# Sending one split output block: which rows go through which transfer engine, and by which queue

## The chip, the core and the metric

The kernel runs on one core of a Trainium2 chip. The core has five instruction engines: TensorE (PE, matmuls into PSUM), VectorE (DVE), ScalarE (ACT), GpSimd (POOL) and SyncE (SP). Data moves between HBM and the on-chip memory SBUF through 16 transfer engines, which serve two queues here: SyncE's (q1 in the profile) and GpSimd's (q0). A transfer is cut into packets, each transfer engine works through its own share, and when its share has landed it counts the transfer's semaphore up by one. "Landing records" in this text are the times of these counts, sixteen for a transfer.

The metric is the time of one execution on the device in microseconds. Before the change three runs took 299.66, 299.67 and 300.48 us, a median of 299.67 us.

## What is computed

```python
def setup_inputs():
    batch, n_heads, seq_t, seq_s, channels = 8, 12, 512, 512, 64
    return {
        "x": np.random.randn(batch, n_heads, seq_t, channels).astype(np.float32),
        "y": np.random.randn(batch, n_heads, seq_s, channels).astype(np.float32),
    }

def reference(x, y):
    return np.einsum('bhtc,bhsc->bhts', x, y).astype(np.float32)
```

For each of the 96 pairs of batch and head, the 512 x 64 matrix x is multiplied with the transposed 512 x 64 matrix y. Inputs are 25.2 MB, the output is 100.7 MB.

## The kernel before

**Tiles and stages.** The 96 heads are worked on as 6 groups of 16. One group of x, and one of y, is one load of 2 MB into one of five slots (`load`, L156). `compress` (L165) rounds a loaded slot to bf16, `mix` (L189) and `transposes` (L204) bring the channels onto the partitions. The output leaves as 48 blocks of 2 MB; block `o` has 128 rows of 4096 numbers (16 KB), a row for each partition. For each block `result` (L363) has TensorE make two half blocks in two PSUM tiles (`products`, `four`) and ScalarE copy them to a slot (L370), and then `store` (L356) has SyncE send the slot to HBM (L361). A slot is filled again when its store has landed. The matmuls run in one loop, `all_products` (L244), while the other engines' instructions are written out one after another. `emit` (L111) records what each instruction reads and writes and puts the waits in front of it.

**The split block.** One block, number `SPLIT` = 41 of 0 to 47, is sent in two parts. `store` sends only its odd rows, 64 runs of 16 KB, as half a store (1024 KB, L359 to L361). Its 64 even rows are computed again in another layout and sent apart, by transfers that do not use all sixteen transfer engines alike:

- `pick` (L266) has VectorE collect the columns of x for these rows into `picked`, in 18 banks of 96 columns. The table `APART` (L53) has one entry for each group of rows: `p` is the first partition that the group gets (further ones follow in steps of 4), `many` the number of partitions, and `first` the first row. Each partition gets `MANY` = 2 runs, run `j` of partition `e` being row `first + j * many + e`. From row `REST` = 60 on, four rows are cut into 16 units of 1024 numbers (4 KB), one for each of 16 partitions, in the last two banks (L283).
- `pieces` (L291) has TensorE multiply the banks behind blocks 41 and 45 (`BEHIND`) and VectorE and ScalarE copy the results into `kept`.
- `send` (L331) issues the transfers. Entries with `many` = 4 go by SyncE (two transfers of 4 partitions with 2 runs, 128 KB each), those with 11 by GpSimd (two of 11 partitions with 2 runs, 352 KB each). The 16 units go by SyncE as one transfer (64 KB, L349).
- `step` (L320) is a small transfer by GpSimd's queue, of 5 rows with two pieces of 64 bytes. It reads x into a tile that nobody uses. It is issued once at the start (L395) and once between the two 11-row transfers.

**What follows.** Behind all this work stands the end of a block of instructions whose engines are gathered by GpSimd (`tile_critical`, L388): every engine ends with a drain, and GpSimd then lets SyncE issue the last store, that of block 47 (L439). While that store runs, VectorE waits for all other transfers (L433).

Of the kernel before, what the change touches and what calls it, by code (L numbers as in the profile page):

```python
# [9 lines left out]
def kernel(  # L10
# [22 lines left out]
    nc = tc.nc  # L33
    B, H, T, C = x.shape
    _, _, S, _ = y.shape
# [4 lines left out]
    NG = B * H // G  # L40
    NH = 2 * NG
    V = G // 4
    K = 8
    E = R // K
    D = 32
# [4 lines left out]
    MANY = 2  # L50
    BANKS = MANY * K + 2
    BEHIND = {SPLIT: range(3), SPLIT + 4: range(3, 5)}
    APART = ((32, 4, 0), (33, 4, 8), (52, 11, 16), (53, 11, 38))  # L53
    REST = 60
    TURN = 4 * V
    fp32 = mybir.dt.float32
    bf16 = mybir.dt.bfloat16
# [4 lines left out]
    xv = x.rearrange("b h t c -> (b h t c)").rearrange("(g p n) -> g p n", p=P, n=R * C)  # L62
# [18 lines left out]
    spare = sb.tile([P, 2, D], fp32, name="spare")  # L81
# [7 lines left out]
    def need(name, points, known_by=None, held=None):  # L89

        best = {}
        for p, v in points:
            if known[name].get(p, 0) < v:
                best[p] = max(best.get(p, 0), v)
        for p, v in list(best.items()):
            if any(snaps[q, w].get(p, 0) >= v for q, w in best.items() if q != p):
                del best[p]
        if known_by is not None:
            assert all(p in dict(known_by) and v <= dict(known_by)[p] for p, v in best.items())
        for p, v in best.items():  # L100
            if held is not None:
                held.append((p, v))
            elif known_by is None:
                engines[name].wait_ge(sems[p], v)  # L104
            known[name][p] = v
            for q, w in snaps[p, v].items():
                known[name][q] = max(known[name].get(q, 0), w)
# [3 lines left out]
    def emit(name, make, reads=(), writes=(), dma=None, lane=None, known_by=None, held=None):  # L111

        points = [writer[r] for r in (*reads, *writes) if r in writer]
        points += [v for w in writes for v in readers.get(w, ())]
        if name == "pool" and name in ticks:
            points.append((name, ticks[name]))
        need(name, points, known_by, held)
        p, step = (lane or name, 1) if dma is None else (f"dma{dma}", 16)
        if p not in sems:
            sems[p] = tc.alloc_semaphore(p)  # L120
        if held is not None:
            held.append(make)
        elif make is not None:
            make().then_inc(sems[p], step)
        at = (p, ticks.get(p, 0) + step)
        ticks[p] = at[1]
        snaps[at] = {**known[name], p: at[1]}
        if dma is None:
            for q in lanes.get(name, (name,)):
                snaps[at][q] = ticks.get(q, 0)  # L130
        for r in reads:
            readers.setdefault(r, []).append(at)
        for w in writes:
            writer[w], readers[w] = at, []
# [21 lines left out]
    def load(n):  # L156
        i = loaded[n] = slot()
        emit(
            "sp",
            lambda: nc.sync.dma_start(slots[i], (yv if n % 2 else xv)[n // 2]),  # L160
            writes=both(i),
            dma=i,
        )
# [98 lines left out]
    kept = keep[:, :BANKS * S].bitcast(fp32)  # L262
    runs = kept[:, :MANY * K * S].rearrange("p (j n) -> p j n", j=MANY)
    picked = keep[:, 3 * NG * R // 2 * D:].bitcast(bf16)[:, :BANKS * 96].rearrange("p (b m) -> p b m", b=BANKS)

    def pick():  # L266

        half, h = divmod(SPLIT % (2 * V), V)
        xT = xTs[half].bitcast(bf16).rearrange("p (k h q u) -> p k h q u", k=K, h=V, u=2)[:, :, h, :, 0]
        under = [("yb", 1, b, ch) for b in range(NG - 3, NG - 1) for ch in range(2)]  # L270
        for at, (p, many, first) in enumerate(APART):
            emit(
                "dve",
                lambda: nc.vector.tensor_copy(  # L274
                    picked[:, :MANY * K, p:p + 4 * many - 3:4].rearrange("p (j k) e -> p j k e", j=MANY),
                    xT[:, :, first:first + MANY * many].rearrange("p k (j e) -> p j k e", j=MANY),
                ),
                [("xT", half)],
                [("picked", at)] + (under if at == 0 else []),
            )  # L280
        emit(
            "dve",
            lambda: nc.vector.tensor_copy(  # L283
                picked[:, MANY * K:, 32::4].rearrange("p b (r c) -> p b r c", c=4),
                xT[:, :, REST:].rearrange("p (c b) r -> p b r c", b=2),
            ),
            [("xT", half)],
            [("picked", len(APART))],
        )

    def pieces(o):  # L291
# [4 lines left out]
        for g in BEHIND[o]:  # L296
# [3 lines left out]
            def make(banks=banks, pm=pm):  # L300
# [8 lines left out]
            emit(  # L309
                "pe", make, [("picked", at) for at in range(len(APART) + 1)] + [("yT", half)],  # L310
                [("pm", pm)], held=held[o],
# [5 lines left out]
            )  # L317
        need("pe", [v for pm in range(2) for v in readers[("pm", pm)]], held=held[o])

    def step():  # L320

        emit(
            "pool",
            lambda: nc.gpsimd.dma_start(  # L324
                spare[0:17:4, :, :D // 2], xv[0, 0:5].rearrange("p (a b c) -> p a b c", a=2, c=D)[:, :, 0, :D // 2]
            ),
            writes=["spare"],
            dma="step",
        )

    def send():  # L331

        dst = ov[SPLIT // V, SPLIT % V][:, 0]
        for p, many, first in APART:
            name = "sp" if many == 4 else "pool"
            if first == APART[-1][2]:
                step()
            emit(
                name,
                lambda: engines[name].dma_start(  # L340
                    dst[first:first + MANY * many].rearrange("(j e) n -> e j n", j=MANY),
                    runs[p:p + 4 * many - 3:4],
                ),
                reads=[("xk", g) for g in range(NG - 1)],
                dma="corner" if name == "sp" else "side",
            )
        emit(
            "sp",
            lambda: nc.sync.dma_start(  # L349
                dst[REST:].rearrange("r (c n) -> (r c) n", c=4), kept[32:93:4, MANY * K * S:]  # L350
            ),
            reads=[("xk", g) for g in range(NG - 1)],
            dma="corner",
        )

    def store(o, s):  # L356
# [6 lines left out]
    def result(o, s):  # L363

        for k in range(0, K, 4):
            pm = k // 4
            products(o, k)
            emit(
                "act",
                lambda: nc.scalar.activation(  # L370
                    slots[s][:, k * S:(k + 4) * S], pms[pm].rearrange("p j s -> p (j s)"), COPY
                ),
                [("pm", pm)],
                [("slot", s, pm)],
                lane=f"ev{(2 * o + pm) % TURN}",
            )
        if o < V * NH - 1:
            store(o, s)
# [9 lines left out]
    with tc.tile_critical(sync_engine=mybir.EngineType.Pool) as work:  # L388
        for at in (TURN - 2, TURN - 1):
            sems[f"ev{at}"] = tc.alloc_semaphore(f"ev{at}")  # L390
            ticks[f"ev{at}"] = 1
            nc.scalar.sem_inc(sems[f"ev{at}"], 1)
        for g in range(SLOTS):
            load(g)
        step()  # L395
        for half, name in enumerate(("dve", "pool")):
            emit(
                name,
                lambda: engines[name].memset(xbs[half], 0.0),  # L399
                writes=[("xb", half, part) for part in range(4)],  # L400
            )
        front = []
        for n in range(2 * NG):
            if n == 11:
                result(3, slot())
            compress(n)
            mix(n // 4, "pool", n % 4)
            if n == 4:
                transposes(0)
            if n < 5:  # L410
                load(n + SLOTS)
            elif n in (6, 8):
                load(n // 2 + 7)
            elif n < 10:
                front.append(slot())
            if n > 7 and n < 11:
                result(n - 8, front[n - 8])
            if n == 9:
                transposes(1)
        prepare(2)  # L420
        for o in range(V, V * NH):
            result(o, slot())
            if o in BEHIND:
                pieces(o)
            if o == max(BEHIND):
                send()
            if o % V == V - 1:
                prepare(o // V + 2)
            if o == SPLIT - V - 1:
                pick()  # L430
        all_products()
# [43 lines left out]
```

## Time and profile before

| what | us |
|---|---|
| median of three runs | 299.67 |
| profiled execution | 299.64 |
| its span, first to last instruction | 297.8 |
| ACT busy | 214.2 |
| DVE busy | 159.5 |
| PE busy | 140.5 |
| POOL busy | 58.5 |

The span is what the profiler saw between the first and the last instruction; the execution lasts 1.84 us longer. Busy shares are averages over the whole span, so that the last 30 us, where the split block is sent, have to be read by themselves: in the timeline (start, length, engine, line) and in the issues of transfers, which the page lists with size and median time from the issue to the landing:

```profile
out_dram<-slot SPq DMA_DIRECT2D x47, 2048.0 KB, 20.8
out_dram<-slot SPq DMA_DIRECT2D x1, 1024.0 KB, 18.4
out_dram<-keep POOLq DMA_DIRECT2D x2, 352.0 KB, 9.6
out_dram<-keep SPq DMA_DIRECT2D x2, 128.0 KB
out_dram<-keep SPq DMA_DIRECT2D x1, 64.0 KB
spare<-in_x_dram POOLq DMA_DIRECT2D x2, 0.6 KB, 7.5
```

A store takes some 20 us to land because three or four others stand before it in SyncE's queue; one 2 MB store lands every 4.9 us.

### The profile page before, as it was taken

Reading aid. Unit: us, or ns where it says so; the run is one execution under the profiler, and the core shown is the slowest. Engines: PE = TensorE matmul, PEld = TensorE weight load, DVE = VectorE, ACT = ScalarE, POOL = GpSimd, SP = SyncE. Lnnn points to the kernel's source line nnn. Section 1 sums busy time; section 2 is a strip of 40 time slices with the busy share of each in tenths; the row PEclk is TensorE's granted clock in tenths of the full one; section 3 lists DMA queues with packets and bytes.
Section 4 is the critical chain, followed back from the end, with each engine's and each line's share of the span. In section 5 each row is a group of like instructions: output and inputs, shape, how many; then the busy total and the mean of one; then the engine's idle time right before and its main releaser. Section 6 shows DMA issues by size and latency. Waiting matters only on the chain.

```text
span 297.8 us, 1269 instructions
## 1 busy us (share of the span) xinstructions
PE 140.5 (47%) x396; PEld 38.2 (13%) x402; DVE 159.5 (54%) x81; ACT 214.2 (72%) x111; POOL 58.5 (20%) x27
## 2 busy tenths in 40 slices
PE   0000040456656553866565667556657556754200
PEld 0000010111111111111111111111111112211000
DVE  2157897999839594906809339167095435103000
ACT  1665676999999988686868686868686865597700
POOL 3399999991000000000000000000000000002000
PEclk9999999978799998565786775786775686799855
DMA  7999999999999999999999999999999999999997
GB/s 271 433 427 436 429 427 429 427 422 442 429 431 422 440 429 430 425 438 429 431 425 439 429 431 429 433 429 427 429 436 425 429 427 427 425 422 431 416 429 315
DMA packets 8794, 125.85 MB, mean 423 GB/s; under 512 B 1100, under 2 KB 1100, under 8 KB 1116
## 3 DMA queue, kind: packets, MB, share of 16 engines
q1 hardware_dynamic: 8632, 125.11, 98.8%
q0 software_dynamic: 160, 0.72, 0.6%
q14 instruction: 2, 0.02, 0.0%
HBM read 25.17 MB, written 100.66 MB: 422 GB/s over the span
## 4 chain that ended last, share of the span: by engine, by line
DMA 54%; ACT 28%; issue 5%; PE 4%; DVE 3%; ACTq 1%; SPq 0%; POOLq 0%
DMA out_dram<-slot 41%; ACT slot L370 25%; DMA slot<-in_y_dram 7%; DMA slot<-in_x_dram 6%; DVE keep L144 3%; ACT keep L142 3%; PE pm L238 2%; PE pm L303 1%; ACTq L388 1%; SPq L160 0%; ACTq L104 0%; SPq L470 0%; POOLq L388 0%; POOLq L459 0%
## 5 line engine op out<-in xcount | busy, mean ns | idle before, releaser
L370 ACT ACTIVATE slot<-pm 128x2048 f32<-128x2048 f32 x96 | 173.8, 1897 | 41.6 <-DMA out_dram<-slot 35.3
L238 PE MATMUL pm<-yT,xT 128*128 128x512 bf16 x378 | 134.1, 496 | 133.6 <-ACT slot L370 91.9
L209 DVE STREAM_TRANSPOSE xT<-xb 128x2048 uint32<-128x2048 uint32 x12 | 46.7, 3895 | 68.5 <-PE pm L238 66.2
L238 PEld LDWEIGHTS pm<-yT,xT 128*128 128x128 bf16 x384 | 35.9, 113 | 231.7 <-ACT slot L370 129.1
L142 ACT ACTIVATE keep<-slot 128x4096 bf16<-128x4096 f32 (+1 forms) x12 | 36.5, 3041 | 21.2 <-DMA slot<-in_x_dram 16.1
L144 DVE COPY xb<-keep 32x2048 bf16<-32x2048 bf16 x36 | 46.9, 1302 | 1.0
L144 DVE CAST keep<-slot 64x2048 bf16<-64x2048 f32 x12 | 36.2, 3015 | 16.9 <-DMA slot<-in_y_dram 16.7
L340 POOL DMA_DIRECT2D out_dram<-keep x2 | 1.1, 566 | 204.4 <-ACT keep L142 204.4
L144 POOL COPY xb<-keep 32x2048 bf16<-32x2048 bf16 x12 | 36.2, 3021 | 9.0 <-ACT keep L142 8.2
L218 DVE STREAM_TRANSPOSE yT<-keep 128x1024 uint32<-128x1024 uint32 x12 | 23.1, 1926 | 0.0
L144 DVE COPY keep<-pm 96x2048 f32<-96x2048 f32 x3 | 6.9, 2286 | 24.7 <-PE pm L303 24.7
L144 POOL CAST keep<-slot 64x2048 bf16<-64x2048 f32 x6 | 17.8, 2974 | 1.3 <-DMA slot<-in_y_dram 0.8
L303 PE MATMUL pm<-yT,keep 128*96 128x512 bf16 x18 | 6.4, 500 | 4.3 <-ACT slot L370 4.3
L142 ACT ACTIVATE keep<-pm 96x2048 f32<-96x2048 f32 (+1 forms) x2 | 2.9, 1448 | 2.8 <-PE pm L303 2.8
L303 PEld LDWEIGHTS pm<-yT,keep 128*96 128x96 bf16 x18 | 2.3, 151 | 8.1 <-issue 3.6
L399 DVE MEMSET xb<- 128x2048 uint32 x1 | 1.8, 1765 | 1.4 <-PEq L459 1.4
L142 ACT ACT_TABLE_LOAD x1 | 1.3, 1283 | 1.0 <-PEq L459 1.0
L399 POOL MEMSET xb<- 128x2048 uint32 x1 | 1.8, 1824 | 0.0
L324 POOL DMA_DIRECT2D spare<-in_x_dram x2 | 1.2, 620 | 1.2 <-POOLq L388 1.2
L274 DVE COPY keep<-xT 128x64 bf16<-128x64 bf16 (+1 forms) x4 | 0.8, 322 | 0.0
L283 DVE COPY keep<-xT 128x32 bf16<-128x32 bf16 x1 | 0.3, 260 | 0.0
L459 POOL MEMSET const-float32-0.0<- 128x1 f32 x1 | 0.1, 93 | 0.2 <-issue 0.2
(3 smaller groups left out, 0.3 us busy)
## 6 DMA issues: line engine op xcount, KB each, us to landing
out_dram<-slot SPq DMA_DIRECT2D x47, 2048.0 KB, 20.8
slot<-in_x_dram SPq DMA_DIRECT2D x6, 2048.0 KB, 17.6
slot<-in_y_dram SPq DMA_DIRECT2D x6, 2048.0 KB, 20.8
out_dram<-slot SPq DMA_DIRECT2D x1, 1024.0 KB, 18.4
out_dram<-keep POOLq DMA_DIRECT2D x2, 352.0 KB, 9.6
out_dram<-keep SPq DMA_DIRECT2D x2, 128.0 KB
out_dram<-keep SPq DMA_DIRECT2D x1, 64.0 KB
spare<-in_x_dram POOLq DMA_DIRECT2D x2, 0.6 KB, 7.5
```

Of the source, the lines that this page charges most:

```text
L142: lambda: nc.scalar.activation(dst, src, COPY)
L144: else engines[name].tensor_copy(dst, src),
L209: lambda: nc.vector.transpose(xTs[half].rearrange("p (k r e) -> p k e r", k=K, e=E), xbs[half].rearrange("p (k e c) -> p k e c", k=K, e=E),),
L218: lambda: nc.vector.transpose(yTs[half].rearrange("p (r j) -> p j r", r=D), ybs[half][b].rearrange("p (j c) -> p j c", c=D),),
L238: last = nc.tensor.matmul(pms[pm][:, b, :], xT[:, 4 * pm + b, h, :], yT[:, h * S:(h + 1) * S], start=True, stop=True,)
L274: lambda: nc.vector.tensor_copy(picked[:, :MANY * K, p:p + 4 * many - 3:4].rearrange("p (j k) e -> p j k e", j=MANY), xT[:, :, first:first ...
L303: last = nc.tensor.matmul(pms[pm][:96, b, :], picked[:, bank, :], yT[:, h * S:(h + 1) * S], start=True, stop=True,)
L324: lambda: nc.gpsimd.dma_start(spare[0:17:4, :, :D // 2], xv[0, 0:5].rearrange("p (a b c) -> p a b c", a=2, c=D)[:, :, 0, :D // 2]),
L340: lambda: engines[name].dma_start(dst[first:first + MANY * many].rearrange("(j e) n -> e j n", j=MANY), runs[p:p + 4 * many - 3:4],),
L370: lambda: nc.scalar.activation(slots[s][:, k * S:(k + 4) * S], pms[pm].rearrange("p j s -> p (j s)"), COPY),
L388: with tc.tile_critical(sync_engine=mybir.EngineType.Pool) as work:
L399: lambda: engines[name].memset(xbs[half], 0.0),
```

## The change

The table `APART` gets five entries and two new columns: `j`, the first run of the group's partitions, and `runs_each`, how many runs each has. The first two groups (rows 0 to 15, by SyncE) stay as they are. Rows 16 to 27 now go as 12 partitions with one run, rows 28 to 38 as 11 partitions with one run, rows 39 to 60 as 11 partitions with two runs, each as one transfer by GpSimd. The last three rows (61 to 63) are cut into 12 units of 4 KB and go by GpSimd too, where before four rows went as 16 units by SyncE. `step` becomes `to_engine(n, at)`, of `n` rows instead of 5: with 4 rows at the start, with 5, 5 and 4 rows in front of the last three transfers. The two 352 KB transfers thus become one of 192 KB, one of 176 KB and one of 352 KB, and the 64 KB transfer one of 48 KB. GpSimd issues seven transfers behind the matmuls instead of three, SyncE two instead of three. `pick` has one copy more, and its last one covers 12 partitions instead of 16.

```diff
-    APART = ((32, 4, 0), (33, 4, 8), (52, 11, 16), (53, 11, 38))
-    REST = 60
+    APART = ((32, 4, 0, 2, 0), (33, 4, 0, 2, 8), (48, 12, 0, 1, 16), (52, 11, 1, 1, 28), (53, 11, 0, 2, 39))
+    REST = 61
...
-        for at, (p, many, first) in enumerate(APART):
+        for at, (p, many, j, runs_each, first) in enumerate(APART):
             emit(
                 "dve",
                 lambda: nc.vector.tensor_copy(
-                    picked[:, :MANY * K, p:p + 4 * many - 3:4].rearrange("p (j k) e -> p j k e", j=MANY),
-                    xT[:, :, first:first + MANY * many].rearrange("p k (j e) -> p j k e", j=MANY),
+                    picked[:, j * K:(j + runs_each) * K, p:p + 4 * many - 3:4].rearrange(
+                        "p (j k) e -> p j k e", j=runs_each
+                    ),
+                    xT[:, :, first:first + runs_each * many].rearrange("p k (j e) -> p j k e", j=runs_each),
                 ),
...
-                picked[:, MANY * K:, 32::4].rearrange("p b (r c) -> p b r c", c=4),
+                picked[:, MANY * K:, 48::4].rearrange("p b (r c) -> p b r c", c=4),
...
-    def step():
+    def to_engine(n, at=0):
 
         emit(
             "pool",
             lambda: nc.gpsimd.dma_start(
-                spare[0:17:4, :, :D // 2], xv[0, 0:5].rearrange("p (a b c) -> p a b c", a=2, c=D)[:, :, 0, :D // 2]
+                spare[at:at + 4 * n - 3:4, :, :D // 2],
+                xv[0, 0:n].rearrange("p (a b c) -> p a b c", a=2, c=D)[:, :, 0, :D // 2],
             ),
-            writes=["spare"],
+            writes=[("spare", at)],
             dma="step",
         )
 
     def send():
 
         dst = ov[SPLIT // V, SPLIT % V][:, 0]
-        for p, many, first in APART:
+        ready = [("xk", g) for g in range(NG - 1)]
+        for at, (p, many, j, runs_each, first) in enumerate(APART):
             name = "sp" if many == 4 else "pool"
-            if first == APART[-1][2]:
-                step()
+            if name == "pool" and first > 16:
+                to_engine(16 - many, at - 2)
             emit(
                 name,
                 lambda: engines[name].dma_start(
-                    dst[first:first + MANY * many].rearrange("(j e) n -> e j n", j=MANY),
-                    runs[p:p + 4 * many - 3:4],
+                    dst[first:first + runs_each * many].rearrange("(j e) n -> e j n", j=runs_each),
+                    runs[p:p + 4 * many - 3:4, j:j + runs_each],
                 ),
-                reads=[("xk", g) for g in range(NG - 1)],
+                reads=ready,
                 dma="corner" if name == "sp" else "side",
             )
-        emit(
-            "sp",
-            lambda: nc.sync.dma_start(
-                dst[REST:].rearrange("r (c n) -> (r c) n", c=4), kept[32:93:4, MANY * K * S:]
+        to_engine(4, 3)
+        emit(
+            "pool",
+            lambda: nc.gpsimd.dma_start(
+                dst[REST:].rearrange("r (c n) -> (r c) n", c=4), kept[48:93:4, MANY * K * S:]
             ),
-            reads=[("xk", g) for g in range(NG - 1)],
-            dma="corner",
+            reads=ready,
+            dma="side",
         )
...
-        step()
+        to_engine(4)
```

## The prediction

> **What bounds the kernel now.** I read the busy slices and the queue table of the page first, then who waited for whom on SyncE, then the timeline of the last 27 us, then the landing records of the last transfers (one time per transfer engine, without its number).
>
> ```profile
> span 297.8 us, 1269 instructions
> DMA  7999999999999999999999999999999999999997
> q1 hardware_dynamic: 8632, 125.11, 98.8%
> q0 software_dynamic: 160, 0.72, 0.6%
> ```
>
> The sixteen transfer engines are full from the first slice to the last; compute is under this (ACT 72%, PE 47%). SyncE's and GpSimd's queues (q1, q0) share them. One 16 KB packet, a run, takes 98.8% x 16 x 297.8 us x 16 KB / 125.11 MB, some 0.61 us; the packet records have a median of 0.611 us on q1 and 0.6155 us on q0. Time can therefore go only by levelling the engines at the end, and come by loading the one that ends last.
>
> ```profile
> 272.29 2.06 SPq L340 DMA_DIRECT2D out_dram<-keep  x2
> 272.86 0.57 POOL L340 DMA_DIRECT2D out_dram<-keep  x1 [204.37 <-ACT keep L142]
> 273.44 0.56 POOL L324 DMA_DIRECT2D spare<-in_x_dram  x1
> 274.00 0.56 POOL L340 DMA_DIRECT2D out_dram<-keep  x1
> 274.39 1.32 SPq L349 DMA_DIRECT2D out_dram<-keep  x1
> 277.34 0.59 SPq L361 DMA_DIRECT2D out_dram<-slot  x1
> 285.72 0.56 SPq L439 DMA_DIRECT2D out_dram<-slot  x1
> ```
>
> This is where the split block goes out; L439 is the very last store, and it waited for GpSimd:
>
> ```profile
> SPq L439 <- POOLq L388: 7.3, 1, 7.3
> ```
>
> GpSimd's closing instruction (L388, a drain, 274.01 to 285.42) ended 0.21 us behind the last landing of GpSimd's transfers (285.21). So SyncE issues the last store only when all of GpSimd's transfers have landed.
>
> The landing records give the balance. Up to 276.3 us one engine is late: it landed at 276.27, the fifteen others by 274.46. The two side transfers of L340 landed on 5 engines early (279.20 to 279.53, then 281.87 to 282.47) and on 11 late (280.38 to 280.90, 284.52 to 285.21). The store of block 45, which follows, landed on four engines at 283.99 to 284.32, on one at 286.16, on eleven at 286.37 to 286.84. So eleven engines carried four runs each (4 x 0.6155 = 2.46 us late), four carried none yet, and the slow one carries none at all. SyncE's two four-row transfers land next on four engines alone (285.23 to 285.56 for the first), so those are the first four, the slow one is the fifth. The end: one landing at 296.08, fifteen from 296.34 to 296.81, the first of them the fifth engine by this account. Behind 296.81 lie 1.04 us to the end of the span and 1.84 us to the execution's 299.64 us, which is 0.03 us under the median of the runs.
>
> **The change, part by part.**
>
> *Picking rows (VectorE).* The four copies of L274 (two at 238 ns for 64 elements, two at 406 ns for 176) and one of 260 ns become six, of 64, 64, 96, 88, 176 and 24 elements. Between those two forms an element costs 1.5 ns: 476 + 286 + 274 + 406 + 260 = 1.70 us against 1.55 us, 0.15 us more at 226.6 us. The transposes after them wait 7.49 us for PE (234.91). Cost 0; without that idle time 0.15 us.
>
> *SyncE.* One issue of 1.32 us (L349) goes. SyncE then waits until 277.3 us for ScalarE. Gain 0.
>
> *GpSimd.* Three late transfers become seven, in the order 12 rows of one run, a mover of 5 rows, 11 rows of one run, a mover of 5, 11 rows of two runs, a mover of 4, 12 rows of 4 KB. Issuing costs 4 x 0.56 = 2.2 us more; GpSimd has no work behind it. They stand ahead of the drain and so of the last store.
>
> *Small packets.* Each added transfer puts two packets of about 9 ns on every engine: 4 x 2 x 9 = 0.07 us.
>
> *Bytes per engine.* This decides. Before, in runs of 16 KB: engines 1 to 4 carry 4 (by SyncE), the fifth none, engines 6 to 16 carry 4 (by GpSimd), and a 4 KB unit each. SyncE's two four-row transfers stay, and pin 4 runs on engines 1 to 4. What GpSimd's new transfers add depends on where they start. The trace has on that queue only transfers with two counted steps a side (11 rows of two runs, 5 rows of two pieces), and these go to as many engines as rows, behind where the last one stopped. Transfers with one counted step (rows of one contiguous piece), as three of the new ones are, it shows only on q1: the halved store of 64 runs (18.4 us to land) and the 16 units of L349, all over the sixteen from the first one. So there are two ends:
> - by the nearest row of the same queue, the one-step transfers follow on from the mover: 12 on engines 5 to 16, 11 on 6 to 16, the units on 5 to 16. Engines 6 to 16 carry 4 runs and a unit as before, the fifth 1 run more, engines 1 to 4 a unit less.
> - by the nearest row of the same shape, they take all sixteen from the first: 12 rows on engines 1 to 12, 11 rows on 1 to 11, units on 1 to 12, and they don't move the starting place. Movers of 4 (at the start), 5 and 5 then put the start of the 11 x 2 transfer at engine 15, and it takes 15, 16 and 1 to 9. Engines 1 to 4 carry 4 + 1 + 1 + 2 = 8 runs and a unit, engines 5 to 9 carry 4, 10, 11, 15 and 16 carry 2, 12 one, 13 and 14 none.
>
> I take the second, as the likelier end: the change keeps the queue and makes the shape new, and in all rows shown it is the shape that sets how many engines a transfer gets (4 rows four, 11 rows eleven, 16 and 64 rows sixteen). [...]
>
> *Sum.* Engines 1 to 4 get 4 x 0.6155 = 2.46 us more. They end between 296.34 and 296.81 now; I take 296.7 for the latest of the four: 296.7 + 2.46 + 0.07 = 299.2. With 1.04 and 1.84 us behind it: **302.1 us**. The others end before: the fifth at 296.08 + 2.46 = 298.5. The last store comes late (below), but engines 1 to 4 have older work until 291.2 + 2.46 = 293.6, so its first packet, 1.02 us behind the issue as with the first load (0.89 to 1.91), is late only if the issue is behind 292.6.
>
> **The rivals.**
>
> *A, the rows go where the change says.* The fifth engine ends at 296.08 + 0.62 + 0.07 = 296.8, engines 6 to 16 stay at 296.81, the first four lose 0.16 us. 299.7 us, no change. For it: both of GpSimd's shapes in the trace turn as this needs. Against: neither has the new shape.
>
> *B, A with a late last store.* On engines 6 to 16 GpSimd's packets come one between two of SyncE's: from the first (278.0) to the last increment (284.17) lie 4 x 0.615 + 6 x 0.611 = 6.1 us. Afterwards there are 15 such packets, so up to 14 gaps: 4 x 0.615 + 0.16 + 14 x 0.611 = 11.2 us, or 2.4 us less if each increment follows its data at once (one of two did). The drain ends 2.7 to 5.1 us later, the last store is issued at 288.4 to 290.8 and its packets come at 289.4 to 291.8, while SyncE's queue runs dry at 291.1 to 291.6. This costs 0 to 0.7 us: 299.7 to 300.4. It decides once the drain is over 4.4 us later; to be over 0.9 us, it needs GpSimd's transfers to be prepared more slowly than the trace shows (the third stood ready 3 us behind the first). 300.6 us.
>
> *C, half of the misplacement.* The one-step rows start at engine 1, but the 11 x 2 transfer stays on 6 to 16. Engines 1 to 4 get 2 x 0.6155 = 1.23 us more: 300.9 us. It needs that the one-step rows move the start after all.
>
> *D, the other side: the first four engines set the end.* Placed as in A, they lose their 4 KB, 0.16 us, and if they alone are at 296.81 the time falls to 299.5. Levelling can't give more than the landings allow: the mean of the sixteen is 296.5, so 0.3 us. Against it: the latest of block 45's store (286.84) belong to the engines with side runs.
>
> **How the numbers follow.** Forecast 302.1 (chance 0.64), C 300.9 (0.12), B over 0.9 us 300.6 (0.05), A with B's small cost 299.7 to 300.4 (0.16), D 299.5 (0.03). What this kernel's measurement can tell from no change is 0.3%, 0.9 us. Slower: 0.64 + 0.12 + 0.05 = 0.81; A is within; D at -0.2 us is within as well, but I leave 0.02 for a gain that the landings don't show: same 0.17, faster 0.02. The range 300.3 to 302.8 holds the three slower cases. Its low end is C's time less 0.6 us: 0.4 us if engines 1 to 4 are the early ones of the last landings (296.34), and 0.2 us that B may be shorter. Its high end is the forecast with the top landing (296.81) and one run more, 0.1 + 0.6 us.
>
> **What would show it.** Right: the last store's landings spread over 2 us or more instead of 0.7, four engines last, near 299.2; mean GB/s of the whole lower, the last slices of DMA below 9 with some engines idle; the first side transfer's late landings are 12, among them engines that the four-row transfers use, so that those land over 1 us later than at 285.2 to 285.6. The last store's wait for L388 grows from 7.3 to some 10 to 12 us in every case. Wrong: landings at 296 to 297 within 0.8 us (A), or all sixteen late together (B). A gain over 0.3 us would break the account of full engines.

## The result and the profile after

The changed kernel takes 303.45 us (five runs, 303.14 to 303.97) against 299.67 us before: a ratio of 1.0123, 95% interval 1.0111 to 1.0134. It is slower, as forecast, but by 3.8 us instead of 2.4, and 0.65 us above the range.

The span ends 1.04 us behind the last landing, as before. The execution outlasts its span by 2.07 us (303.40 against 301.33 us in the profiled execution), where the kernel before has 1.79 us (299.64 against 297.85; with the span rounded to 297.8 it reads 1.84).

The page of the changed kernel, span, busy slices and queues:

```profile
span 301.3 us, 1273 instructions
DMA  7999999999999999999999999999999999999986
GB/s 278 422 437 431 420 437 428 420 433 431 428 439 420 437 431 427 437 422 437 433 424 438 424 435 433 422 435 431 424 442 422 422 433 431 422 420 415 361 335 289
q1 hardware_dynamic: 8600, 125.05, 97.9%
q0 software_dynamic: 272, 0.79, 0.9%
```

The loss is all in the last slices: the rate falls to 361, 335 and 289 GB/s while the engines still count as full up to the last two. GpSimd's queue (q0) holds the engines for 0.9% of their time instead of 0.6%, for 0.79 MB instead of 0.72. The same stretch in windows, first of the kernel before, then of the changed one; the last two numbers of a row are the busy share of the transfer engines and what they moved, in GB/s:

```profile
278.00:284.00 6.00, 0.41 (x2) 0.00 (x0) 0.00 (x0) 2.86 (x2) 0.00 (x0) 0.79 1.03 434
284.00:290.00 6.00, 0.00 (x0) 0.00 (x0) 0.00 (x0) 0.00 (x0) 0.00 (x0) 0.50 1.00 423
290.00:296.00 6.00, 0.00 (x0) 0.00 (x0) 0.00 (x0) 0.00 (x0) 0.00 (x0) 0.50 0.98 418
```

```profile
278.00:284.00 6.00, 1.30 (x4) 0.15 (x1) 0.00 (x0) 3.12 (x2) 0.00 (x0) 0.50 1.03 353
284.00:290.00 6.00, 0.00 (x0) 0.00 (x0) 0.00 (x0) 0.00 (x0) 0.00 (x0) 0.50 1.00 370
290.00:296.00 6.00, 0.00 (x0) 0.00 (x0) 0.00 (x0) 0.00 (x0) 0.00 (x0) 0.50 0.78 332
```

Two different losses. From 278 to 290 us all engines are busy but move a sixth less: packets take longer. From 290 to 296 us a fifth of the engines' time is idle: some have nothing left to do. The packet records say the same: GpSimd's 16 KB packets take 0.62 us before (mean) and 0.90 us after, at most 1.66; SyncE's between 277 and 290 us take 0.62 and 0.69 us.

SyncE's timeline and its wait for the last store, in the changed kernel:

```profile
277.50 0.59 SPq L366 DMA_DIRECT2D out_dram<-slot  x1
293.42 0.58 SPq L444 DMA_DIRECT2D out_dram<-slot  x1
```

```profile
SPq L444 <- POOLq L393: 14.9, 1, 14.9
```

The last store is issued at 293.42 us instead of 285.72, because GpSimd's drain ends (293.12) behind the landing of its seventh transfer (292.74). The landing records: block 46's store lands from 291.88 to 295.45 us, 3.6 us apart (0.7 before); the last store from 299.91 to 300.30, 0.4 us apart. Engines that had nothing left all start again with the last store, and those that had most end with them.

### The profile page after: what moved, and what is told of

The parts are those of the page before. It is cut to its first block, busy times and chain, and to the rows that moved or that the text cites. A ratio compares the mean times of both kernels' runs of the same rounds, so it can differ in the third digit from the quotient of the medians.

```text
span 301.3 us, 1273 instructions
## 1 busy us (share of the span) xinstructions
PE 141.7 (47%) x396; PEld 38.4 (13%) x402; DVE 159.4 (53%) x82; ACT 214.3 (71%) x111; POOL 60.8 (20%) x31
## 4 chain that ended last, share of the span: by engine, by line
DMA 54%; ACT 27%; issue 5%; PE 4%; DVE 3%; SPq 0%; ACTq 0%; POOLq 0%
DMA out_dram<-slot 41%; ACT slot L375 24%; DMA slot<-in_y_dram 7%; DMA slot<-in_x_dram 6%; DVE keep L144 3%; PE pm L238 3%; ACT keep L142 3%; PE pm L305 1%; SPq L160 0%; ACTq L104 0%; SPq L475 0%; POOLq L393 0%; POOLq L464 0%
## 5 line engine op out<-in xcount | busy, mean ns | idle before, releaser
L344 POOL DMA_DIRECT2D out_dram<-keep x3 | 1.6, 550 | 204.5 <-ACT keep L142 204.5
L326 POOL DMA_DIRECT2D spare<-in_x_dram x4 | 2.6, 644 | 1.2 <-POOLq L393 1.2
L274 DVE COPY keep<-xT 128x64 bf16<-128x64 bf16 (+3 forms) x5 | 0.8, 277 | 0.0
L354 POOL DMA_DIRECT2D out_dram<-keep x1 | 0.5, 546 | 0.0
```

The lines of the kernel that those rows point to most:

```text
L274: lambda: nc.vector.tensor_copy(picked[:, j * K:(j + runs_each) * K, p:p + 4 * many - 3:4].rearrange("p (j k) e -> p j k e", j=runs_each), ...
L326: lambda: nc.gpsimd.dma_start(spare[at:at + 4 * n - 3:4, :, :D // 2], xv[0, 0:n].rearrange("p (a b c) -> p a b c", a=2, c=D)[:, :, 0, :D / ...
L344: lambda: engines[name].dma_start(dst[first:first + runs_each * many].rearrange("(j e) n -> e j n", j=runs_each), runs[p:p + 4 * many - 3: ...
L354: lambda: nc.gpsimd.dma_start(dst[REST:].rearrange("r (c n) -> (r c) n", c=4), kept[48:93:4, MANY * K * S:]),
```

## The experiments

Eight kernels. Theory P says that the bytes went to the wrong engines, theory L that the drain holds back the last store whatever the bytes do.

**Give the one-run groups a second step.** The halves of a run are kept apart in SBUF (a group's halves in banks 0 to 3 and 8 to 11, or 4 to 7 and 12 to 15), so that a transfer can't be written with one step. The part that sends the runs; the collecting of the columns and the units are changed to match:

```diff
-                    dst[first:first + runs_each * many].rearrange("(j e) n -> e j n", j=runs_each),
-                    runs[p:p + 4 * many - 3:4, j:j + runs_each],
+                    dst[first:first + MANY * many].rearrange("(j e) n -> e j n", j=MANY)
+                    if runs_each == 2
+                    else dst[first:first + many].rearrange("e (h n) -> e h n", h=2),
+                    runs[p:p + 4 * many - 3:4]
+                    if runs_each == 2
+                    else runs[p:p + 4 * many - 3:4].rearrange("p j (g n) -> p j g n", g=2)[:, :, j],
...
```

> The changed kernel, but each run of the two one-run groups, and each 4 KB unit, is kept in two halves that lie apart in SBUF, so that these three GpSimd transfers have two counted steps a side like those of the kernel before. Theory P (placement: one-step rows start at transfer engine 1 and double the load of engines 1 to 4): now 12 and 11 rows go to engines 5 to 16 and 6 to 16 as the change says, block 46's landings lie within 1 us instead of 3.6, GpSimd's packets take 0.61 us per 16 KB, and the time is 299.7 to 301.5 us, what is left over 299.7 being the late last store alone (the halves put 3 more packets between SyncE's). Theory L (the seven transfers ahead of the drain make it late, wherever their bytes go): the drain still ends near 293 us and the time stays at 303.0 to 303.7 us.

Measured: 301.63 us, ratio 1.0069 (1.0053 to 1.0086). Block 46 lands from 291.67 to 292.28 us, 0.6 us apart. GpSimd's 16 KB packets, here only the 22 of the two-run group, take 0.62 us. The second side transfer lands on five engines early (282.72 to 283.27) and on eleven late (283.76 to 284.51), the third again on five and eleven. So the placement is that of the change's words, and it was the one-step form that had spoiled it. (The edit also halves the packets of the one-run groups to 8 KB; that wasn't tried apart from the second step.) Most of what is left over the kernel before is a late last store:

```profile
278.55 0.59 SPq L375 DMA_DIRECT2D out_dram<-slot  x1
291.55 0.58 SPq L453 DMA_DIRECT2D out_dram<-slot  x1
```

It is issued at 291.55, and all sixteen engines land together from 298.05 to 298.25, 6.70 us behind the issue and 1.4 us later than in the kernel before; some 0.3 us more lie between the end of the span and the end of the execution. The time is 0.13 us above what P allowed, and far below what L asked for.

**Same placement, fitting partitions.** The landing records carry no engine number. Numbered by which engines land together, as in the prediction (four with SyncE's first four-row transfer, 285.23 to 285.56 us, eleven late ones with each of GpSimd's, from 280.38 and from 284.52), engine 1 + i reads partitions 32 + 4i and 33 + 4i in the kernel before: SyncE's groups start at 32 and 33 on engine 1, GpSimd's at 52 and 53 on engine 6. In the changed kernel the misplaced groups break this: by the placement of the forecast engine 1 reads partitions 48 and 52, and of the two-run group 53 or 61, depending on whether the first row goes to the lowest of the engines taken or to the one at which the transfer starts. Here the one-run groups read partitions 34, 38, ..., the two-run group 35, 39, ... and the units 32, 36, ...: by the same placement, with the first row on the lowest engine, engine 1 + i reads 32 + 4i or one of the next three, all but the last two partitions of the two-run group.

```diff
-    APART = ((32, 4, 0, 2, 0), (33, 4, 0, 2, 8), (48, 12, 0, 1, 16), (52, 11, 1, 1, 28), (53, 11, 0, 2, 39))
+    APART = ((32, 4, 0, 2, 0), (33, 4, 0, 2, 8), (34, 12, 0, 1, 16), (34, 11, 1, 1, 28), (35, 11, 0, 2, 39))
...
-                picked[:, MANY * K:, 48::4].rearrange("p b (r c) -> p b r c", c=4),
+                picked[:, MANY * K:, 32:77:4].rearrange("p b (r c) -> p b r c", c=4),
...
-                dst[REST:].rearrange("r (c n) -> (r c) n", c=4), kept[48:93:4, MANY * K * S:]
+                dst[REST:].rearrange("r (c n) -> (r c) n", c=4), kept[32:77:4, MANY * K * S:]
```

> [...] The bytes on each engine are as in the changed kernel. If the 1.1 us by which my forecast fell short come from engines that read each other's partitions: GpSimd's 16 KB packets fall from a mean of 0.90 to under 0.66 us and the time to 301.7 to 302.5 us. If packets are slow for another reason (two queues on one engine, more transfers in flight): they stay at 0.85 to 0.95 us and the time at 303.1 to 303.7 us.

Measured: 302.60 us (302.56 to 302.67), ratio 1.0095 (1.0078 to 1.0111); 0.1 us above what was expected for the first case. GpSimd's packets take 0.64 us instead of 0.90, none over 0.98; that the two-run group is among the fast ones speaks for the first row on the lowest engine. The windows show the rate coming back; what is missing is only engines without work:

```profile
278.00:284.00 6.00, 0.82 (x4) 0.20 (x2) 0.00 (x0) 3.27 (x2) 0.00 (x0) 0.97 1.05 424
284.00:290.00 6.00, 0.00 (x0) 0.00 (x0) 0.00 (x0) 0.00 (x0) 0.00 (x0) 0.50 0.92 388
```

The landings of block 46 are the clearest picture of the placement in any run, a ladder: two engines at 289.14 and 289.18 us, one at 289.97, two at 290.83 and 291.07, six from 291.69 to 291.88, one at 293.59, four from 294.27 to 294.73. The prediction's loads, in runs of the split block's even rows, are none on two engines, one on one, two on four, four on four and on the fifth, which was late before too, and eight on four. Two of the four engines with two runs land among those with four; by the prediction's placement engines 15 and 16 read partitions 71 and 75 here, next to those of engines 10 and 11 in the kernel before (68, 69 and 72, 73), which may be why. The last store lands on eleven engines from 296.69 to 296.83, on one at 298.47, on four at 299.15, 299.16, 299.34 and 299.60: the fifth engine at 298.5 as predicted, engines 1 to 4 last. The eleven land 6.7 us behind the issue of the last store (290.11), the floor that it sets.

**The kernel before, partitions shifted.**

```diff
-    APART = ((32, 4, 0), (33, 4, 8), (52, 11, 16), (53, 11, 38))
+    APART = ((32, 4, 0), (33, 4, 8), (34, 11, 16), (35, 11, 38))
```

> The kernel before with one edit: the two 11-row groups lie on partitions 34, 38, ... and 35, 39, ... instead of 52, 56, ... and 53, 57, .... Engines, bytes, transfers and order are unchanged. If an engine that reads another engine's partitions slows both: GpSimd's 16 KB packets take over 0.75 us instead of 0.616 and the time rises to 300.2 to 301.7 us. If partitions don't matter: 0.616 us and 299.5 to 299.9 us.

Measured: 302.76 us, ratio 1.0102 (1.0085 to 1.0119), with the same rows in the same transfers. Packets of the side transfers take 0.88 us. The two queues from 277 to 290 us, in this kernel and then in the kernel before (packets, MB, share of the engines):

```profile
q1 hardware_dynamic: 311, 3.98, 81.3%
q0 software_dynamic: 128, 0.72, 19.0%
```

```profile
q1 hardware_dynamic: 359, 4.77, 86.8%
q0 software_dynamic: 128, 0.72, 13.4%
```

The same 128 packets of GpSimd's hold the engines for 19.0% instead of 13.4%, and SyncE's stores lose too: 3.98 MB in 81.3% of 16 x 13 us are 0.70 us for 16 KB, 4.77 MB in 86.8% are 0.62 us. The effect is larger than I had expected (3.0 us instead of 0.5 to 2). With the run above it makes a square: partitions from 34 on are fast when engine 1 reads the first of them (0.64 us) and slow when engine 6 does (0.88); partitions from 52 on are fast for engine 6 (0.62) and slow for engine 1 (0.90, the mean with the group from 48 on). So it is the pairing of engine and partition that counts, not either by itself.

**The last store made late, nothing else.** Eight movers behind the last side transfer of the kernel before (`step` gets the number of rows and the place as arguments):

```diff
+        for at in (32, 33, 34, 35, 48, 49, 50, 51):
+            step(4, at)
...
```

> The kernel before with eight more movers (4 rows of two 64-byte pieces) behind GpSimd's last side transfer: no bytes worth counting, but the drain and so the last store come later. At two packets each behind one of SyncE's, five of them take the time until SyncE's queue runs dry at 291.3 us and the rest go fast: drain at 292 to 293, issue at 292.3 to 293.3, last landing 6.7 us behind the issue, time 301.9 to 302.9 us. If the last store isn't what the drain holds back: 299.6 to 300.1 us.

Measured: 303.29 us, ratio 1.0117 (1.01 to 1.0134), 0.4 us more than expected, since the drain ended at 293.3 us. The windows show the hole itself:

```profile
290.00:293.00 3.00, 0.00 (x0) 0.00 (x0) 0.00 (x0) 0.00 (x0) 0.00 (x0) 0.50 0.50 208
293.00:294.50 1.50, 0.00 (x0) 0.00 (x0) 0.00 (x0) 0.00 (x0) 0.00 (x0) 0.50 0.00 0
294.50:300.00 5.50, 0.00 (x0) 0.00 (x0) 0.00 (x0) 0.00 (x0) 0.00 (x0) 0.50 0.90 381
```

The last store is issued at 293.63 and lands until 300.31, 6.68 us later. By this price a last landing at 296.8 needs an issue by 290.1 us. The mechanism of L is real; the next runs say what it is worth in the changed kernel.

**The last store not late.** The store of block 47 is issued like the others, ahead of the drain, in the changed kernel, in the kernel before and in the two-step kernel:

```diff
-        if o < V * NH - 1:
-            store(o, s)
+        store(o, s)
...
-    last = nc.sync.dma_start(ov[NH - 1, V - 1], slots[made_slots[-1]])
...
```

> The kernel before with the same edit as last_store_early, a measure of what the edit itself costs: the last store isn't late in the kernel before, so the last landing stays at 296.5 to 297.0 us and the time rises by the waits that now stand behind the last landing, 0.2 to 0.8 us: 299.9 to 300.5 us.

Measured: 300.69 us, ratio 1.0034 (1.0023 to 1.0046), slightly more than expected. The last landing is 296.86 us as without the edit, and the span ends 2.0 us behind it instead of 1.04: VectorE's waits for the transfers, about 0.1 us each, and its closing steps now follow the last landing. So the edit costs 0.95 us.

> The changed kernel with one edit: the store of block 47 is issued with the other stores, ahead of GpSimd's drain, so that nothing holds it back; the wait for all transfers then stands behind it. Theory P (engines 1 to 4 hold too much and are slowed by their partitions): in the changed kernel the latest engine of block 46's store landed at 295.45 us and that of the last store 4.85 us later, without a gap, so the last landing stays at 300.0 to 300.5 us and the time at 303.0 to 304.0 us (a longer way from the last landing to the end included, which the next run measures). Theory L (the late last store alone): the last landing falls to 297 us or less and the time to 300.5 us or less.

Measured: 304.37 us, ratio 1.0156 (1.0139 to 1.0173), above the 304.0 us allowed; 303.45 us and the 0.95 us that the edit itself costs are 304.40. The last landing is 300.18 us, against 300.30 with the late store. Taking the wait away gains 0.1 us: the loaded engines work without a gap until then. But the late store alone would have put the last landing at 293.42 + 6.7 = 300.1 us, whatever the loads. In the changed kernel the two limits lie within 0.1 us of each other, and each hides the other.

> Both edits together, two_step_rows and last_store_early. If nothing but the late last store (issued at 291.55 us, landed at 298.25) kept two_step_rows at 301.63 us: the last landing falls to 296.6 to 297.2 us and the time to that of before_last_store_early within 0.4 us. If the seven transfers cost the transfer engines time of their own: the last landing stays over 297.5 us.

Measured: 301.23 us, ratio 1.0049 (1.0033 to 1.0066). The last landing falls from 298.25 to 297.07, the time is 0.54 us above the kernel before with the same edit, a little over the 0.4 allowed: 0.2 us by the last landing, the rest between the end of the span and the end of the execution (2.08 against 1.80 us). Once the bytes are where the change wants them, the late store is the bound, and without it nothing is gained either: 297.07 against 296.86.

**One part of the change alone: the units by GpSimd's queue**, in the kernel before.

```diff
         emit(
-            "sp",
-            lambda: nc.sync.dma_start(
+            "pool",
+            lambda: nc.gpsimd.dma_start(
                 dst[REST:].rearrange("r (c n) -> (r c) n", c=4), kept[32:93:4, MANY * K * S:]
             ),
...
-            dma="corner",
+            dma="side",
```

> The kernel before with one part of the change: the 16 units of 4 KB go by GpSimd's queue instead of SyncE's, as one more transfer ahead of the drain. [...] The drain ends 1.2 to 2.5 us later than 285.4, the last store is issued at 287 to 288.3, still ahead of 291, and the time stays at 299.5 to 299.9 us. If moving a transfer to GpSimd's queue costs by itself: 300.2 us or more.

Measured: 299.91 us, ratio 1.0005 (0.9996 to 1.0015): no change that can be told. The last store is issued at 287.36 us, so what moving the units to that queue costs can't be told from nothing while the issue stays ahead of 290 us.

None of the eight beats the kernel before.

## Why the prediction was half right

- **Bytes per engine: right.** The forecast took the row of the same shape, all sixteen engines from the first, over the row of the same queue. The two-step run, which differs in the form of these transfers, moves the bytes back, and the landings with fitting partitions show the loads step by step, the fifth engine at 298.47 for 298.5. With one-step rows the loads fit a start at the first engine (block 46's ladder with fitting partitions, 289.14 to 294.73 us); with two-step rows the second side transfer landed on five engines early (282.72 to 283.27) and on eleven late (283.76 to 284.51), as when each transfer goes on where the last one stopped. How rows of any other form are dealt out no run shows.
- **"Engines 1 to 4 get 4 x 0.6155 = 2.46 us more": this step failed, in the size of its term.** The 0.6155 us came from a kernel in which engines and partitions are paired as 32 + 4i to 1 + i. Mispaired, GpSimd's packets took 0.90 us, and SyncE's in the same stretch 0.69 instead of 0.62. The last landing moved by 300.30 - 296.81 = 3.5 us instead of 2.5. Between the changed kernel and the one with fitting partitions it differs by 300.30 - 299.60 = 0.7 us, of which 0.1 us is the late last store (300.18 without it); the medians differ by 0.85 us. Without this dearer term the time would be 302.60 us, inside the range, whose upper end allowed for one run more, not for dearer runs.
- **"Each added transfer puts two packets of about 9 ns on every engine: 0.07 us": perhaps too small; this stays open.** Of the 160 packets that GpSimd's queue has for its four transfers before, 44 are runs, 10 the movers' pieces and 106 have 4 or 8 bytes and take 9 ns: 128 times 4 bytes, two for each of sixteen engines and four transfers. With fitting partitions the last landing is at 299.60 us where the sum has 299.2. In the two-step run engines 1 to 4 carry no additional run, yet SyncE's first four-row transfer lands on them at 285.68 to 285.96 instead of 285.23 to 285.56, 0.4 us later, where the kernel before with the early last store, which has the same transfers there, is 0.1 us later (285.39 to 285.69). So the small packets seem to cost more than their length. But the fifth engine gets them too, and with fitting partitions it lands at 298.47, where 296.08 + 2.46 = 298.54 leaves nothing for them. GpSimd's 16 KB packets at 0.64 instead of 0.6155 us are 0.1 us for four runs. Where the rest of the 0.4 us comes from isn't shown.
- **"1.84 us behind it", taken over unchanged: 0.2 us too small.** What lies between the end of the span and the end of the execution is 2.07 us in the changed kernel. In the profiled executions it is 2.04 to 2.08 us in all five kernels with the new GpSimd transfers, 1.79 or 1.80 us in the three with the old ones, 1.91 with the units by GpSimd and 1.94 with eight movers. What it consists of no run shows. The three terms, 0.7, 0.4 and 0.2 us, are 1.3 of the 1.35 us between forecast and measurement.
- **Picking rows and SyncE's issue, at nothing: nothing speaks against it.** The two-step kernel picks as many groups and has SyncE's issue away too, and with the early last store its last landing is only 0.2 us behind (297.07 against 296.86). They weren't tried alone.
- **The last store "is late only if the issue is behind 292.6": the condition came, the cost hardly did.** The issue was at 293.42, since the slower packets delay GpSimd's transfers as well (290.11 with fitting partitions). But they also keep the loaded engines in block 46 until 295.45 instead of the forecast's 293.6, so the late issue was worth 0.1 us, as the run without it shows.
- **Rival A, the rows go where the change says, with B's late store:** its placement isn't what the changed kernel does. Made to happen, it cost more than the 0 to 0.7 us written there: 298.25 - 296.81 = 1.4 us. The point at which B decides (a drain over 4.4 us later than 285.42, an issue behind 290.1) was right; the drain came 5.8 us later, with three packets more on the queue than B had counted.
- **Rival C** would have left engines 1 to 4 at six runs and the time at 300.9; four engines 2.5 us behind the rest speak for eight. **Rival D** never had its condition.
- **What would show it:** the last slices lost rate and fell below 9, and SyncE's four-row transfers landed from 288.60 us on, over 3 us later than before. Four engines last can be seen with fitting partitions alone; in the changed kernel itself block 46's landings spread from 291.88 to 295.45 without a step, and the last store's are 0.4 us apart, not over 2, because the late issue lets the idle engines start together and end near the loaded ones. All sixteen late together is the sign that the prediction gave for B; only block 46's landings and the run with the early last store tell the two apart here. SyncE's wait grew to 14.9 us, not to 10 to 12.

## What to carry to other kernels

Which transfer engines the rows took hung here on the form of the access pattern (block 46 landed 3.6 us apart with one counted step, 0.6 us with two and smaller packets): before building a balance on it, look at how many engines land early, for that very pattern and on that queue. When bytes move to another engine, price them with a row in which the engine reads the same partitions, not just the same packet size: here 16 KB took 0.90 us instead of 0.62. Before adding a transfer to a queue, ask what is issued behind a wait for that queue: the barrier here, which waits for GpSimd's transfers, turned additional transfers into a delay of the store issued behind it (from 285.72 to 287.36 us with one more, to 293.63 with eight movers); the delay was free up to 4.4 us, and then cost one for one (with eight movers the issue came 3.5 us behind 290.1, the last landing 3.5 us behind 296.8).

## What was not expected of the hardware

With other partitions for the same engines, packets of both queues took longer. GpSimd's 16 KB packets took 0.62 us paired as in the kernel before, 0.90 us in the changed kernel (single ones up to 1.66) and 0.88 us in the kernel before with its two groups shifted by 18 partitions; SyncE's went from 0.62 to 0.69 and 0.70 us. The shift alone cost the kernel before 3.0 us of 299.8. Fast were the groups that start at partitions 32 to 35 on engine 1 and at 52 and 53 on engine 6 (0.62 to 0.64 us): for engine 1 + i, partitions 32 + 4i to 35 + 4i. Why the pairing counts is not shown: the records give neither the engine nor the partitions of a packet. That engines read at the same time what others read, and that both lose by it, was my explanation alone.
